# Gate-and-up product with four of eight pairs on seven products, a weight sum formed by an accumulating transfer, and the token scale folded into silu's result

## The chip, the cores and the metric

The kernel runs on one core of a Trainium2 chip. Its metric is the device time of one launch in microseconds (us). TensorE (PE) multiplies, VectorE (DVE) and ScalarE (ACT) work elementwise, GpSimd (POOL) here mostly issues transfers, and SyncE (SP) issues the loads. SBUF is the memory on the core; PSUM holds what PE sums up, in banks of 128 x 512 floats.

## The reference

A decoder of two layers on 256 tokens with 2048 features, all in float32. Layer 0 mixes tokens by a dilated sliding-window attention, layer 1 by a latent attention; the change leaves both alone. Each layer ends with a feed-forward block (FFN):

```python
def swiglu(xn, w_gu, w_down):
    g, u = jnp.split(xn @ w_gu, 2, axis=-1)
    return (jax.nn.silu(g) * u) @ w_down
...
h = h + swiglu(rms_norm(h, ffn_norm_g[layer]), ffn_w_gu[layer], ffn_w_down[layer])
```

`w_gu` is 2048 x 11264 (5632 columns of gate, then 5632 of up), `w_down` 5632 x 2048. `rms_norm` multiplies each token by one number, the token scale below.

## The kernel before

**Products.** Every float32 operand is split into two fp32r halves, `hi` (a rounded copy, by ACT) and `lo` (what is left, by DVE). A product of two blocks is then three matmuls: hi by hi, hi by lo, lo by hi (L595 to L597, called by `mul` in `mixed`). Each has 128 tokens against 512 weight columns.

**Weights.** `WeightStream` passes all weights through as units of 128 x 2048 floats (1 MB): rows 2kp and 2kp+1 (in blocks of 128) of two bands of 512 columns, one *pair* kp. `load` brings a unit into one of three `raw` buffers by transfers that SP issues; `split` makes `hi` and `lo` of it (L146 on ACT, L147 on DVE), two units ahead of use; `begin` does the first part of the third unit ahead (its early steps: the sums and the cast of `hi`).

**Eight or seven.** A pair is a 2 x 2 block product: two halves of the tokens, two bands of columns, two row blocks. In the form "eight" that is eight products, 24 matmuls, summed in two accumulators (`acc`, one for the gate or left band, one for the up or right band). In the form "seven" it is done by sums and differences with seven products, 21 matmuls. This needs sums of the weights (L168 adds two quarters of `raw` in place, L169 and L170 form three more, `sums`, by DVE), their halves `th` (ACT) and `tl` (DVE), sums of the activations (`forms`, `forms_h`, made by `sums`, L565 on), and four PSUM banks, `pb`, which gather over all seven-pairs of a group. After the last seven-pair the four banks are cast (L635 on ACT; L636, L637 and L642 on DVE) into the tiles `gate` and `up` (in down groups `left` and `right`). `raw` has three buffers, `hi` and `lo` three each, `th`, `tl` and `sums` one each.

**Groups.** One call of `mixed` is a group. `ffn` does the hidden columns in three parts of 16, 16 and 12 blocks (`FFN_PARTS`): first a gate-and-up group of eight pairs for every four blocks, then the down groups of that part. Per layer these are 11 gate-and-up groups and 5 down groups. The first gate-and-up group of a layer has eight products in every pair; the other ten have seven in the pairs of `SEVEN = (2, 4, 6)`. At a gate-and-up group's end, `close` adds the accumulator to what the banks gave (L861), ACT applies silu with the token scale (L866), and DVE multiplies `up` by the token scale and by `gate` (L870). One pair later (`later.put(1, turned)`) `turned` transposes `up` on PE (L429) into `hT`, the left operand of the down groups. Down groups end by adding into the residual `h`, one part by DVE, one by transfers on POOL's queue that add in memory (L890, to `h` from `gate` and `up`).

**Order.** In the FFN, DVE and ACT run in the order in which the code is written (`tc.manual_schedule(engines=ORDERED)`). PE's order is chosen by the scheduler of the framework. Units are numbered by their pair below: unit 1 of a group is the load of pair 1.

## Time and profile before

| | us |
|---|---|
| median of 3 runs (2654.10 to 2654.79) | 2654.57 |
| the profiled execution | 2654.07 |
| its span (first to last instruction) | 2652.0 |

| | busy us | share of the span |
|---|---|---|
| PE | 2637.8 | 99% |
| DVE | 2183.1 | 82% |
| ACT | 1324.0 | 50% |
| POOL | 29.7 | 1% |

The mean granted clock is 0.998. The loads move 492.65 MB and take 56.5% of the time of the 16 DMA engines; the queue that POOL feeds moves 10.49 MB. A gate-and-up group takes 42.67 us, a down group of eight pairs 41.70 us. The share of an engine is an average over the whole program, so the question of which engine has room has to be asked for a single group, where the change is.

### The profile page before, as it was taken

Reading aid. Unit: us, or ns where it says so; the run is one execution under the profiler, and the core shown is the slowest. Engines: PE = TensorE matmul, PEld = TensorE weight load, DVE = VectorE, ACT = ScalarE, POOL = GpSimd, SP = SyncE. Lnnn points to the kernel's source line nnn. Section 1 sums busy time; section 2 is a strip of 40 time slices with the busy share of each in tenths; the row PEclk is TensorE's granted clock in tenths of the full one; section 3 lists DMA queues with packets and bytes.
Section 4 is the critical chain, followed back from the end, with each engine's and each line's share of the span. In section 5 each row is a group of like instructions: output and inputs, shape, how many; then the busy total and the mean of one; then the engine's idle time right before and its main releaser. Section 6 shows DMA issues by size and latency. Waiting matters only on the chain.

```text
span 2652.0 us, 32612 instructions
## 1 busy us (share of the span) xinstructions
PE 2637.8 (99%) x12856; PEld 2214.1 (83%) x12856; DVE 2183.1 (82%) x2590; ACT 1324.0 (50%) x1404; POOL 29.7 (1%) x32
## 2 busy tenths in 40 slices
PE   9999999999999999999999999999999999999998
PEld 7888888888888888888888888888888888888887
DVE  6776777777677789998899898688789998998996
ACT  5444444534444455554554455565555554554554
POOL 0000000000000000000000000000000000000000
PEclk9999999999999999999999999999999999999999
DMA  7544645554554555567567757544565676657765
GB/s 263 188 165 160 206 159 175 186 180 159 174 189 161 191 185 197 190 209 235 191 198 218 219 181 223 166 152 136 159 206 180 201 222 207 207 183 230 217 209 159
DMA packets 310265, 506.27 MB, mean 191 GB/s; under 512 B 15112, under 2 KB 118240, under 8 KB 309728
## 3 DMA queue, kind: packets, MB, share of 16 engines
q1 hardware_dynamic: 304048, 492.65, 56.5%
q0 software_dynamic: 5440, 10.49, 2.5%
q8 instruction: 100, 1.64, 0.2%
q10 hardware_dynamic: 624, 1.07, 0.1%
q14 instruction: 53, 0.43, 0.0%
HBM read 491.57 MB, written 2.10 MB: 186 GB/s over the span
## 4 chain that ended last, share of the span: by engine, by line
PE 95%; DVE 2%; issue 1%; ACT 1%; DMA 1%; SPq 0%; POOL 0%; POOLq 0%; DVEq 0%; ACTq 0%
PE acc L595 16%; PE acc L596 16%; PE acc L597 16%; PE acc L489 15%; PE acc L492 8%; PE bank L597 4%; PE bank L595 4%; PE bank L596 3%; PE acc L509 3%; PE acc L510 3%; PE acc L508 3%; PE bank L429 1%; PE bank L689 1%; DVE lo L147 1%; PE bank L704 1%
## 5 line engine op out<-in xcount | busy, mean ns | idle before, releaser
L146 ACT CAST hi<-raw 128x2048 fp32r<-128x2048 f32 (+3 forms) x622 | 882.9, 1445 | 897.5 <-PE acc L489 268.7
L147 DVE TENSOR_TENSOR lo<-raw,hi 128x2048 fp32r<-128x2048 f32 (+3 forms) x622 | 1057.1, 1710 | 252.6 <-ACT hi L146 228.2
L595 PE MATMUL acc<-hi,xT_f 128*128 128x512 f32 x996 | 391.1, 393 | 0.0
L596 PE MATMUL acc<-lo,xT_f 128*128 128x512 f32 x996 | 389.3, 391 | 0.0
L597 PE MATMUL acc<-hi,xT_f 128*128 128x512 f32 x996 | 388.3, 390 | 0.0
L489 PE MATMUL acc<-xT_a,hi 128*128 128x512 f32 x1536 | 379.1, 396 | 0.0
L489 PEld LDWEIGHTS acc<-xT_a,hi 128*128 128x128 f32 x1536 | 281.8, 188 | 53.7
L595 PEld LDWEIGHTS acc<-hi,xT_f 128*128 128x128 f32 x996 | 187.1, 188 | 40.5 <-ACT gate L866 0.8
L597 PEld LDWEIGHTS acc<-hi,xT_f 128*128 128x128 f32 x996 | 187.1, 188 | 39.8
L596 PEld LDWEIGHTS acc<-lo,xT_f 128*128 128x128 f32 x996 | 187.1, 188 | 39.0 <-DVE lo L147 0.4
L147 DVE TENSOR_TENSOR tl<-sums,th 128x1536 fp32r<-128x1536 f32 x104 | 182.4, 1754 | 39.7 <-ACT th L146 39.7
L492 PEld LDWEIGHTS acc<-xT_a,lo 128*128 128x128 f32 x1536 | 196.9, 191 | 7.5
L492 PE MATMUL acc<-xT_a,lo 128*128 128x256 f32 x1536 | 199.3, 283 | 0.0
L146 ACT CAST th<-sums 128x1536 fp32r<-128x1536 f32 x104 | 154.2, 1483 | 67.6 <-PE acc L597 45.2
L595 PE MATMUL acc<-hi,hT 128*128 128x512 f32 x412 | 161.4, 392 | 0.0
L596 PE MATMUL acc<-lo,hT 128*128 128x512 f32 x412 | 160.9, 391 | 0.0
L597 PE MATMUL acc<-hi,hT 128*128 128x512 f32 x412 | 160.7, 390 | 0.0
L170 DVE TENSOR_TENSOR sums<-raw,sums 128x1024 f32<-128x1024 f32 x104 | 127.4, 1225 | 3.4
L595 PEld LDWEIGHTS acc<-hi,hT 128*128 128x128 f32 x412 | 77.4, 188 | 16.5
L597 PEld LDWEIGHTS acc<-hi,hT 128*128 128x128 f32 x412 | 77.4, 188 | 16.4
L596 PEld LDWEIGHTS acc<-lo,hT 128*128 128x128 f32 x412 | 77.4, 188 | 16.1
L508 PE MATMUL acc<-hi,xT_a 128*128 128x512 f32 x192 | 76.6, 399 | 0.0
(341 smaller groups left out, 4053.4 us busy)
## 6 DMA issues: line engine op xcount, KB each, us to landing
raw<-in_ffn_w_gu_dram SPq DMA_DIRECT2D x352, 512.0 KB, 4.5
raw<-in_a_w_qkv_dram SPq DMA_DIRECT2D x119, 1024.0 KB, 4.8
raw<-in_ffn_w_down_dram SPq DMA_DIRECT2D x152, 512.0 KB, 4.7
raw<-in_a_w_qkv_dram SPq DMA_DIRECT2D x50, 512.0 KB, 4.6
raw<-in_a_w_o_dram SPq DMA_DIRECT2D x32, 512.0 KB, 4.8
raw<-in_b_w_o_dram SPq DMA_DIRECT2D x32, 512.0 KB, 4.6
raw<-in_ffn_w_down_dram SPq DMA_DIRECT2D x12, 1024.0 KB, 6.4
raw<-in_b_w_kv_b_dram SPq DMA_DIRECT2D x8, 1024.0 KB, 5.2
```

The lines of the kernel that those rows point to most:

```text
L146: cast = lambda: nc.scalar.copy(out=hi, in_=src)
L147: rest = lambda: nc.vector.tensor_tensor(out=lo, in0=src, in1=hi.bitcast(F32), op=ALU.subtract)
L170: tt(out=w[:, 0::2], in0=v[:, 1::2], in1=w[:, 1].unsqueeze(1).broadcast_to([P, 2, 512]), op=ALU.subtract)
L429: nc.tensor.transpose(out=ps[:, jj * S + t * P:jj * S + (t + 1) * P], in_=srcs[t][:, (j + jj) * P:(j + jj + 1) * P], identity=ident)
L489: mm(out=acc[:, i, :], lhsT=sl(hi, kk), rhs=xT[:, k0 + kk, :], start=first and kk == 0, stop=False)
L492: mm(out=acc[:, i, 0:S], lhsT=sl(lo, kk), rhs=xT[:, k0 + kk, 0:S], start=False, stop=last and kk == nk - 1)
L508: mm(out=acc[:, t, :ncol], lhsT=xh, rhs=rhs(hi, kk), start=st, stop=False)
L509: mm(out=acc[:, t, :ncol], lhsT=xh, rhs=rhs(lo, kk), start=False, stop=False)
L510: mm(out=acc[:, t, :ncol], lhsT=xl, rhs=rhs(hi, kk), start=False, stop=sp)
L595: mm(out=out, lhsT=xh, rhs=wh, start=st, stop=False)
L596: mm(out=out, lhsT=xh, rhs=wl, start=False, stop=False)
L597: mm(out=out, lhsT=xl, rhs=wh, start=False, stop=sp)
```

## The change

It has four parts.

1. `SEVEN` becomes (1, 3, 5, 6): in the ten groups of a layer, four of eight pairs have seven products, 60 matmuls fewer in the whole program. Pairs 5 and 6 follow one another. Where the next pair is a seven too, `mixed` runs the products of the sums first (`summed`, then `plain`).
2. Seven-units of gate-and-up and of down get the form "summed": DVE's add of two quarters (L168) goes. SP loads three pieces (256, 512 and 256 KB), and a fourth transfer, issued by POOL, adds 256 KB from HBM to the first piece where it lies in `raw` (L110 to L113 of the changed kernel; 108 such transfers). The attention's output units keep the add.
3. The cast of the banks keeps its intermediate sum in a small tile `mid`, so `gate` shrinks from three parts of 512 to two, and the last step becomes two subtractions of 512 columns (L652) in place of one of 1024.
4. The token scale goes from DVE to ACT: L870 is gone, ACT multiplies silu's result by the scale (L884, two instructions), and a plain multiply of `up` by `gate` on DVE (L891) stands at the head of `turned`, one pair later than L870 stood. In a layer's first group, which has no L877 (the addition that was L861), ACT copies `up` out of PSUM.

```diff
--- before.py
+++ after.py
@@ -45,7 +45,7 @@
 C_M0, C_M1, C_M2, C_CA, C_SA, C_END = 1024, 1536, 1792, 2048, 2304, 2560
 
 
-SEVEN = (2, 4, 6)
+SEVEN = (1, 3, 5, 6)
 ORDERED = {mybir.EngineType.DVE, mybir.EngineType.Activation}
 SEVEN_O = (4, 6)
 SEVEN_V = ((), (2, 4, 6), (2, 4, 6), (4, 6))
@@ -104,9 +104,14 @@
         while self.n_raw < min(upto, len(self.units)):
             ap, _, form = self.units[self.n_raw]
             t = self.raw_pool.tile([P, 2048], F32, tag="raw", name="raw", bufs=self.raw_bufs)
-            if form in ("eight", "seven"):
+            if form in ("eight", "seven", "summed"):
                 v = t.rearrange("p (k n c) -> p k n c", n=2, c=512)
-                for n in range(2):
+                if form == "summed":
+                    self.nc.sync.dma_start(out=v[:, 0, 0, :], in_=ap[1][:, 0, :])
+                    self.nc.sync.dma_start(out=v[:, :, 1, :], in_=ap[0])
+                    self.nc.sync.dma_start(out=v[:, 1, 0, :], in_=ap[1][:, 1, :])
+                    self.nc.gpsimd.dma_start(out=v[:, 0, 0, :], in_=ap[0][:, 0, :], accum_op=ALU.add)
+                for n in range(0 if form == "summed" else 2):
                     self.nc.sync.dma_start(out=v[:, :, 1 - n, :], in_=ap[n])
                 self.raws[self.n_raw] = t
                 self.n_raw += 1
@@ -158,14 +163,15 @@
         hi, lo = [self.hl_pool.tile([P, 2048], F32R, tag=n, name=n, bufs=self.ahead + 1) for n in ("hi", "lo")]
         if form == "eight":
             return (hi, lo), self.halve(hi, lo, raw)
-        if form == "seven":
+        if form in ("seven", "summed"):
             th, tl = [self.sum_pool.tile([P, 1536], F32R, tag=n, name=n, bufs=1) for n in ("th", "tl")]
             sums = self.sum_pool.tile([P, 1536], F32, tag="sums", name="sums", bufs=1)
             v, w = [t.rearrange("p (i c) -> p i c", c=512) for t in (raw, sums)]
             tt = self.nc.vector.tensor_tensor
 
             def add():
-                tt(out=v[:, 0], in0=v[:, 0], in1=v[:, 1], op=ALU.add)
+                if form == "seven":
+                    tt(out=v[:, 0], in0=v[:, 0], in1=v[:, 1], op=ALU.add)
                 tt(out=w[:, 1], in0=v[:, 0], in1=v[:, 2], op=ALU.subtract)
                 tt(out=w[:, 0::2], in0=v[:, 1::2], in1=w[:, 1].unsqueeze(1).broadcast_to([P, 2, 512]),
                    op=ALU.subtract)
@@ -350,13 +356,13 @@
             for j in range(k0, k0 + n, 4):
                 for kp in range(KD // 2):
                     blocks = [v[:, 2 * kp:2 * kp + 2, b + j * P:b + j * P + 512] for b in (0, FF)]
-                    units.append((blocks, None, "seven" if j > 0 and kp in SEVEN else "eight"))
+                    units.append((blocks, None, "summed" if j > 0 and kp in SEVEN else "eight"))
             v = ffn_w_down[layer].rearrange("(k p) c -> p k c", p=P)
             paired = D // 2 if k0 + n == KF else D
             for c in range(0, paired, 1024):
                 for kp in range(n // 2):
                     blocks = [v[:, k0 + 2 * kp:k0 + 2 * kp + 2, b:b + 512] for b in (c, c + 512)]
-                    units.append((blocks, None, "seven" if kp in SEVEN_DOWN[n] else "eight"))
+                    units.append((blocks, None, "summed" if kp in SEVEN_DOWN[n] else "eight"))
             for c in range(paired, D, 512):
                 for k in range(k0, k0 + n, 4):
                     add_unit(ffn_w_down[layer], k, 4, c, 512)
@@ -609,13 +615,19 @@
                     pb = [bank() for _ in range(4)]
                 at = sums_of.shape[3] - 4
                 y = lambda j: x(1, 0) if j + at < 0 else [sums_of[:, i, h, j + at, :] for h in range(2)]
-                mul(pb[0], x(0, 0), w[:2], 1, st, sp)
-                mul(la[:, 0], x(0, 1), w[:2], 3, first("la0"), False)
-                mul(pb[1], y(0), w[:2], 0, st, sp)
-                mul(ra[:, 0], y(3), w[:2], 2, first("ra0"), False)
-                mul(pb[3], y(2), w[2:], 0, st, sp)
-                mul(pb[2], y(1), w[2:], 1, st, sp)
-                mul(la[:, 1], x(1, 1), w[2:], 2, first("la1"), False)
+                def plain():
+                    mul(pb[0], x(0, 0), w[:2], 1, st, sp)
+                    mul(la[:, 0], x(0, 1), w[:2], 3, first("la0"), False)
+                    mul(pb[1], y(0), w[:2], 0, st, sp)
+                    mul(ra[:, 0], y(3), w[:2], 2, first("ra0"), False)
+
+                def summed():
+                    mul(pb[3], y(2), w[2:], 0, st, sp)
+                    mul(pb[2], y(1), w[2:], 1, st, sp)
+                    mul(la[:, 1], x(1, 1), w[2:], 2, first("la1"), False)
+
+                for part in (summed, plain) if kp + 1 in seven else (plain, summed):
+                    part()
             else:
                 for i, (acc, m) in enumerate(((la, "la"), (ra, "ra"))):
                     for t in range(NT):
@@ -838,7 +850,11 @@
                     sums(xT, kp, forms[:, SEVEN.index(kp)])
 
             def pair_tiles():
-                return [fp.tile([P, n, 512], F32, tag=m, name=m) for m, n in (("gate", NT + 1), ("up", NT))]
+                return [fp.tile([P, NT, 512], F32, tag=m, name=m) for m in ("gate", "up")]
+
+            def pieces(left, right):
+                mid = tmp.tile([P, 2, S], F32, tag="t1", name="mid").rearrange("p a b -> p (a b)")
+                return [left[:, 0], mid, left[:, 1]], right
 
             for part, (k0, n) in enumerate(FFN_PARTS):
                 last = part == len(FFN_PARTS) - 1
@@ -855,7 +871,7 @@
                             later.put(kp + 3, lambda kp=kp: scaled(kp))
                     sc_ = rstd if first else rem
 
-                    def close(i, acc, first=first, both=(gate[:, 0:3:2], up), sc_=sc_):
+                    def close(i, acc, first=first, both=(gate, up), sc_=sc_):
                         d = both[i]
                         if not first:
                             nc.vector.tensor_tensor(out=d, in0=acc, in1=d, op=ALU.add)
@@ -864,18 +880,20 @@
                         def silu():
                             for t in range(NT):
                                 nc.scalar.activation(out=d[:, t], in_=acc[:, t], func=AF.Silu, scale=sc_[:, t:t + 1])
+                            for t in range(NT):
+                                nc.scalar.activation(out=d[:, t], in_=d[:, t], func=AF.Copy, scale=sc_[:, t:t + 1])
                         if i == 0:
                             return silu
-                        for t in range(NT):
-                            nc.vector.scalar_tensor_tensor(out=d[:, t], in0=acc[:, t], scalar=sc_[:, t:t + 1],
-                                                           in1=both[0][:, t], op0=ALU.mult, op1=ALU.mult)
-
-                    def turned(j=j, up=up, hT=hT, seven=SEVEN_DOWN[n], sums_h=sums_h):
+                        if first:
+                            nc.scalar.copy(out=d, in_=acc)
+
+                    def turned(j=j, gate=gate, up=up, hT=hT, seven=SEVEN_DOWN[n], sums_h=sums_h):
+                        nc.vector.tensor_tensor(out=up, in0=up, in1=gate, op=ALU.mult)
                         transposed([up[:, t, :] for t in range(NT)], hT, j, None)
                         for kp in (j // 2, j // 2 + 1):
                             if kp in seven:
                                 sums(hT, kp, sums_h[:, seven.index(kp)])
-                    mixed(xT, KD // 2, () if first else SEVEN, forms, lambda gate=gate, up=up: (gate, up), close)
+                    mixed(xT, KD // 2, () if first else SEVEN, forms, lambda gate=gate, up=up: pieces(gate, up), close)
                     later.put(1, turned)
 
                 for c in range(0, 2 if last else 4, 2):
@@ -885,8 +903,8 @@
                         d = chunks(c + i)
                         nc.vector.tensor_tensor(out=d, in0=acc, in1=d, op=ALU.add)
 
-                    mixed(hT, n // 2, SEVEN_DOWN[n], sums_h, lambda left=left, right=right: (left, right), close)
-                    for i, part_sum in enumerate((left[:, 0:3:2], right)):
+                    mixed(hT, n // 2, SEVEN_DOWN[n], sums_h, lambda left=left, right=right: pieces(left, right), close)
+                    for i, part_sum in enumerate((left, right)):
                         nc.gpsimd.dma_start(out=chunks(c + i), in_=part_sum,
                                             accum_op=ALU.add)
                     if last:
```

What this does to DVE's order where one gate-and-up group (with seven-pairs) meets the next. Before, from the last cast of the banks on (in all such rows: line, operation, output, inputs, shape):

```order
L636 TENSOR_TENSOR gate<-bank,gate 128x512
L637 TENSOR_TENSOR gate<-bank,gate 128x512
L642 TENSOR_TENSOR up<-bank,gate 128x1024
L861 TENSOR_TENSOR gate<-acc,gate 128x2x512
L147 TENSOR_TENSOR lo<-raw,hi 128x2048
L861 TENSOR_TENSOR up<-acc,up 128x1024
L870 SCALAR_TENSOR_TENSOR up<-up,rem,gate 128x512 x2
L168 TENSOR_TENSOR raw<-raw 128x512
L169 TENSOR_TENSOR sums<-raw 128x512
L170 TENSOR_TENSOR sums<-raw,sums 128x2x512
```

Of the changed kernel, DVE at the same place, from the second cast of the banks to the first work after the transposes:

```order
L649 TENSOR_TENSOR gate<-bank,mid 128x512
L652 TENSOR_TENSOR up<-bank,mid 128x512
L652 TENSOR_TENSOR up<-bank,gate 128x512
L175 TENSOR_TENSOR sums<-raw 128x512
L176 TENSOR_TENSOR sums<-raw,sums 128x2x512
L877 TENSOR_TENSOR gate<-acc,gate 128x1024
L152 TENSOR_TENSOR lo<-raw,hi 128x2048
L152 TENSOR_TENSOR tl<-sums,th 128x1536
L877 TENSOR_TENSOR up<-acc,up 128x1024
L152 TENSOR_TENSOR lo<-raw,hi 128x2048
L175 TENSOR_TENSOR sums<-raw 128x512
L176 TENSOR_TENSOR sums<-raw,sums 128x2x512
```

Behind these stands L891, the multiply that completes `up`. So between the addition of `up` and the end of `up` there were no other instructions, and now there are a `lo` (unit 2) and the sums of unit 3; the sums and `tl` of unit 1 stand ahead of them, between the casts of the banks and the addition of `up`.

On PE, whose rows here carry the numbers of the tiles, the rows around the transposes of `up` at such a place were these. `acc_8723` and `acc_8724` are the new group's accumulators, `hi_8643` its unit 0, `hi_8675` its unit 1:

```order
L596 MATMUL acc_8724<-lo_8644,xT_f0_7039 128x512
L597 MATMUL acc_8724<-hi_8643,xT_f0_7039 128x512
L429 MATMUL bank_8758<-ident_95,up_8416 128x128 x4
L429 MATMUL bank_8765<-ident_95,up_8416 128x128 x4
L595 MATMUL acc_8723<-hi_8675,xT_f0_7039 128x512
L596 MATMUL acc_8723<-lo_8676,xT_f0_7039 128x512
```

In the changed kernel the transposes (`up_8445`) come later. The new group's unit 0 is `hi_8679`, unit 1 `hi_8715` with `th_8717`, unit 2 `hi_8759`:

```order
L603 MATMUL acc_8764<-hi_8679,xT_f0_7039 128x512
L601 MATMUL acc_8764<-hi_8715,xT_f0_7039 128x512
L602 MATMUL acc_8764<-lo_8716,xT_f0_7039 128x512
L603 MATMUL acc_8764<-hi_8715,xT_f0_7039 128x512
L601 MATMUL acc_8764<-th_8717,xT_f0_7039 128x512
L602 MATMUL acc_8764<-tl_8718,xT_f0_7039 128x512
L603 MATMUL acc_8764<-th_8717,xT_f0_7039 128x512
L601 MATMUL acc_8764<-hi_8759,xT_f0_7039 128x512
L601 MATMUL acc_8765<-hi_8679,xT_f0_7039 128x512
```

Matmuls of units 1 and 2 that need no bank of `pb` were moved ahead into unit 0's: 42 matmuls stand between the group's first one and the transposes, where 24 stood before.

On ACT the same place was, before, from the cast of a bank on:

```order
L635 COPY gate<-bank 128x512
L146 CAST hi<-raw 128x2048
L866 ACTIVATE gate<-gate,rem 128x512 x2
L146 CAST hi<-raw 128x2048
L146 CAST th<-sums 128x1536
```

And in the changed kernel:

```order
L647 COPY gate<-bank 128x512
L151 CAST hi<-raw 128x2048
L151 CAST th<-sums 128x1536
L882 ACTIVATE gate<-gate,rem 128x512 x2
L884 ACTIVATE gate<-gate,rem 128x512 x2
L151 CAST hi<-raw 128x2048 x2
```

A `th` of unit 1 now stands ahead of silu, and the two multiplies by the token scale behind it, ahead of the `hi` of units 2 and 3.

## The prediction

> **What bounds the kernel now.** I read the page first: its busy line, the slices and the chain.
>
> ```profile
> span 2652.0 us, 32612 instructions
> ...
> PE 2637.8 (99%) x12856; PEld 2214.1 (83%) x12856; DVE 2183.1 (82%) x2590; ACT 1324.0 (50%) x1404; POOL 29.7 (1%) x32
> ...
> DVE  6776777777677789998899898688789998998996
> ...
> PE 95%; DVE 2%; issue 1%; ACT 1%; DMA 1%; SPq 0%; POOL 0%; POOLq 0%; DVEq 0%; ACTq 0%
> ```
>
> PE bounds: it makes 95% of the chain. But DVE reaches nine tenths in the slices of the FFN, so I took the busy time of single groups: first a gate-and-up group (from one L635 copy to the next), then a down group.
>
> ```profile
> 1304.07:1346.74 42.67, 42.67 (x193) 35.20 (x192) 40.38 (x36) 23.06 (x20) 0.00 (x0) 1.00 0.60 196
> 1432.10:1473.80 41.70, 41.70 (x184) 34.33 (x183) 35.77 (x25) 19.81 (x13) 2.40 (x2) 1.00 0.78 231
> ```
>
> Columns are length, PE, PEld, DVE, ACT, POOL, clock, DMA share, GB/s. In gate-and-up DVE works 40.38 of 42.67 us; in down it has 6 us to spare. The clock is 1.00, and DMA is at 0.60 to 0.78. So DVE has some 2 us a group left, just where the change adds to it. Next I looked at where two gate-and-up groups meet, first PE.
>
> ```profile
> 1306.12 0.39 PE L595 MATMUL acc<-th,xT_f 128*128 128x512 f32 x1
> ...
> 1312.08 0.39 PE L597 MATMUL acc<-hi,xT_f 128*128 128x512 f32 x1
> 1312.30 0.39 PE L595 MATMUL acc<-hi,xT_f 128*128 128x512 f32 x1
> ...
> 1317.75 1.03 PE L429 MATMUL bank<-ident,up 128*128 128x128 f32 x8
> ```
>
> From 1306.12 to 1317.75 lie 51 matmuls (3, then 24 and 24): **0.228 us** each. The next group begins at 1312.30, which I call **E**. Its first 24 matmuls run, then the eight transposes of the old group's `up`, at E+5.45, without a wait. DVE at the same place:
>
> ```profile
> 1304.20 2.29 DVE L147 TENSOR_TENSOR lo<-raw,hi 128x2048 fp32r<-128x2048 f32 x1 [1.81 <-ACT hi L146]
> 1306.41 0.68 DVE L636 TENSOR_TENSOR gate<-bank,gate 128x512 f32<-128x512 f32 x1
> 1307.13 0.69 DVE L637 TENSOR_TENSOR gate<-bank,gate 128x512 f32<-128x512 f32 x1
> 1307.85 1.22 DVE L642 TENSOR_TENSOR up<-bank,gate 128x1024 f32<-128x1024 f32 x1
> 1309.78 1.23 DVE L861 TENSOR_TENSOR gate<-acc,gate 128x1024 f32<-128x1024 f32 x1 [0.71 <-PE acc L597]
> 1310.92 2.28 DVE L147 TENSOR_TENSOR lo<-raw,hi 128x2048 fp32r<-128x2048 f32 x1
> 1313.12 1.22 DVE L861 TENSOR_TENSOR up<-acc,up 128x1024 f32<-128x1024 f32 x1
> 1314.44 1.42 DVE L870 SCALAR_TENSOR_TENSOR up<-up,rem,gate 128x512 f32<-128x512 f32 x2
> 1315.78 0.68 DVE L168 TENSOR_TENSOR raw<-raw 128x512 f32<-128x512 f32 x1
> 1316.49 0.69 DVE L169 TENSOR_TENSOR sums<-raw 128x512 f32<-128x512 f32 x1
> 1317.22 1.23 DVE L170 TENSOR_TENSOR sums<-raw,sums 128x1024 f32<-128x1024 f32 x1
> ```
>
> `up` is finished at 1315.86, 1.9 us before PE wants it. From start to start these cost: 0.72 for 512 columns, 1.14 to 1.2 for 1024 (1.27 for L170 with its wait), 2.20 for a `lo`. That spare 1.9 us is what the change spends.
>
> **The change part by part.** *Products.* Each of the 10 changed groups a layer, 20 in all, loses one product of three matmuls: 60 x 0.228 = **-13.6 us**, if PE stays fed. It is the only gain on PE's path.
>
> *DVE's load.* A gate-and-up group loses three raw adds (L168) and gains a fourth pair's sums (0.69 + 1.23) and `tl`:
>
> ```profile
> L147 DVE TENSOR_TENSOR tl<-sums,th 128x1536 fp32r<-128x1536 f32 x104 | 182.4, 1754 | 39.7 <-ACT th L146 39.7
> L146 ACT CAST th<-sums 128x1536 fp32r<-128x1536 f32 x104 | 154.2, 1483 | 67.6 <-PE acc L597 45.2 <-DVE lo L147 18.9 <-DVE sums L170 0.5
> L866 ACT ACTIVATE gate<-gate,rem 128x512 f32<-128x512 f32 x40 | 26.8, 718 | 80.4 <-DVE gate L861 80.4
> ```
>
> 40.38 - 3 x 0.68 + 0.69 + 1.23 + 1.75 + 0.15 (`right` in two halves) - 0.2 (L870's pair becomes one multiply) = 41.96 us, against PE's 42.67 - 0.68 = 41.99. The slack is gone. In down DVE only loses work, which PE covers.
>
> *Where the work lands.* Unit k is the load of pair k. With pair 1 instead of pair 2 in the list, the next group's unit 1 needs sums and `tl` while the old group closes, and L891, the multiply before the transposes, now follows unit 2's `lo` and unit 3's sums (the order rows of DVE above). The chain's start comes first. Unit 6's `th` shares its one buffer with unit 5's, so ACT may write it only after nine matmuls of unit 5, which begins 66 matmuls (15.0 us) before E. These rows price the rest:
>
> ```profile
> 1302.25 1.91 ACT L146 CAST hi<-raw 128x2048 fp32r<-128x2048 f32 x1 [2.19 <-PE acc L597]
> 1311.10 1.34 ACT L866 ACTIVATE gate<-gate,rem 128x512 f32<-128x512 f32 x2 [4.24 <-DVE gate L861]
> 1318.48 1.49 ACT L146 CAST th<-sums 128x1536 fp32r<-128x1536 f32 x1
> 1319.87 1.91 ACT L146 CAST hi<-raw 128x2048 fp32r<-128x2048 f32 x1
> ```
>
> E-15.0 + 2.05 + 0.25 (PE to reader, as 1309.53 to 1309.78 at L861) = E-12.7; `th` and unit 7's `hi` 1.39 + 1.91, two `lo` 4.4: DVE starts the eviction at **E-5.0**, not at E-5.9 as now. Then four evictions 2.88, unit 1's sums 1.99, gate's add 1.14, unit 1's `lo` 2.20 and `tl` 1.67, up's add 1.2, unit 2's `lo` 2.20, unit 3's sums 1.99, L891 1.22: 16.5 us, so `up` is ready at E+11.5. PE has been given 42 matmuls to run ahead of the transposes (counted in its order; 24 before), 9.55 us. It stands for 2.0 us, plus 0.1 for the signal; ACT's `hi` of unit 2, behind two silus and two new copies, ends at about E+5.9 and costs nothing more. After the transposes unit 1 at once wants all four PSUM banks, two of them still being cast: 0 to 0.45, I take 0.3. **2.4 us at each of 14 joints** (7 a layer). Bounds: 1.2, if the chain starts at E-5.9 as now, and 4.4, if a transfer adds 2 us (below).
>
> *Other joints.* Gate to down: no unit-1 sums, but unit 2's sums, `lo` and `tl` stand before L891: 14.5 us from E-5.0 against the same 42 matmuls: 0.3 at six joints. Down to gate: the chain starts at E-5.9 and has no L891; gate's buffer comes free at E+0.2: 0.3 at four. Down to down: hidden.
>
> *First group to second,* once a layer. In this place now:
>
> ```profile
> 1008.65 1.22 DVE L478 TENSOR_TENSOR xT_f<-xT_f,R 128x1024 fp32r<-128x1024 f32 x1
> ...
> 1012.49 0.56 DVE L405 TENSOR_TENSOR forms<-g,forms 128x384 fp32r<-128x384 f32 x1
> 1012.97 2.29 DVE L147 TENSOR_TENSOR lo<-raw,hi 128x2048 fp32r<-128x2048 f32 x1
> 1015.40 1.41 DVE L870 SCALAR_TENSOR_TENSOR up<-acc,rstd,gate 128x512 f32<-128x512 f32 x2 [0.15 <-PE acc L597]
> ```
>
> Scaling one pair and forming its sums takes 4.3 us (1008.65 to 1012.97). L870 ran at 1015.40, ahead of pairs 5 and 6; L891 stands behind the scaling of 3 to 6 with the sums of 3, 5 and 6. By the same prices it ends near 1032.5, where PE, with 59 matmuls from 1015, is ready at about 1028.5; `lo` and `tl` of units 3 to 5 then run late by 0.3 to 1 each. I take **6 us** (bounds 3 and 8), twice.
>
> *The accumulating transfer.* No row shows one from HBM, so I bound it by these:
>
> ```profile
> raw<-in_b_w_kv_a_dram SPq DMA_DIRECT2D x2, 256.0 KB, 2.7
> h<-gate POOLq DMA_DIRECT2D x10, 512.0 KB, 5.9
> h<-up POOLq DMA_DIRECT2D x10, 512.0 KB, 9.5
> L890 POOL DMA_DIRECT2D h<-gate x10 | 12.2, 1218 | 1295.3 <-DVE h L886 700.9 <-issue 594.3
> ```
>
> The first piece lands after 2.7 us, then POOL issues: at most 5.9 us with twice the bytes; less half of the 3.6 us that the second 512 KB adds, 4.1. So 6.8 to 8.6 us from a free buffer to a summed one. The shortest windows from the `lo` that frees it to the first sum are unit 1's (`tl`, two `lo`, four evictions: 9.0) and unit 6's (9.7). It fits, barely: cost 0; with 11 us it would be 2 a joint. Behind the two transfers to `h` (9.5 us, from E+2) unit 4's sum in the second down group lands near E+16; its products begin at E+21, so PE does not notice.
>
> POOL's issue took 1218 ns on average with DVE at work around it; nothing in that row says that DVE holds it up. Here a rule speaks against the change: the Trainium skill, "SBUF — State Buffer", section "Who interferes with whom", says that transfers whose descriptors GpSimd writes wait while DVE holds the port pair that both share, and also that `tensor_tensor`, which is what DVE runs in these stretches, was not seen to stall them. By its first half each issue could slip by up to the 2.29 us of a `lo`, and the third rival's time would come out; by its second half, and by the row, it costs nothing, which is what the sum has.
>
> A second rule bears on the gaps. The granted clock is 1.00 in both group rows above. The Trainium skill, "TensorE: Matmul & The Clock Gate", section "HAM oscillation — how this bites in real kernels", says that TensorE, idle for more than about 3.4 us, falls to half clock, and the section on the gate that it needs about as long to come back. By it the two first groups alone could be hit, if their wait came in one piece: half of 3.4 us lost at each, an estimate of 2692 us instead of my sum. No row of the FFN shows such a gap, so the sum leaves it out.
>
> **Sum.** -13.6 + 14 x 2.4 + 6 x 0.3 + 4 x 0.3 + 2 x 6 = **+35**. The profiled execution took 2654.07 us (its span of 2652.0 and 2.07 around it), 0.5 under the median of the runs shown, so I predict **2689 us**.
>
> **Rivals.** *PE's gain alone*: the moved matmuls cover the whole chain, and 2654.1 - 13.6 = 2640 comes out, faster. It holds if `up` is ready by E+9.5, two microseconds earlier than I find, and if the first groups hide their chain too. For it speaks that PE's order carries 18 more matmuls as cover, and that DVE's load, 41.96 us, still fits PE's 41.99; against it the 16.5 us of rows without a gap. 0.15. *A draw*: joints of about 1 us (DVE starting at E-5.9, the first groups at 1 or 2 us) give back just the gain, 2649 to 2660: 0.1. *A late sum*: first piece, issue and accumulation take some 11 us instead of 8, DVE waits 2 us at each of the 14 joints, +28: 2717. It decides above a window of 9.0 us; the 9.5 us landing of the second transfer to `h` speaks for it, the 5.9 us of the first against it. 0.18. That the change doesn't do what it says is excluded by the order: 60 matmuls fewer.
>
> **How the numbers follow.** Forecast 0.57, late sum 0.18, draw 0.1, gain 0.15. The low end is the draw's, 2649; the forecast with its joints at their lower bounds (1.2 and 3) is 2666. The high end, 2723, is the late sum and a little above; outside lie the gain and the late sum's tail. A measurement here can tell about 0.2%, 5.3 us. Slower by more than that: 0.75; within: 0.1; faster: 0.15.
>
> **What would show it.** Right: gate-and-up groups 44 to 45 us apart instead of 42.67; the transposes of `up` waiting for DVE's L891; DVE over 93% busy in these groups; down groups still 41.8. Wrong: groups at 42.0 (then the cover suffices), or DVE's sums and ACT's `hi` waiting for the transfer on POOL's queue (then the late sum holds).

## The result and the profile after

The changed kernel takes **2705.43 us** (median of four runs, 2699.81 to 2706.38) against 2654.65 us before: 1.0186 times as long, with a 95% interval of 1.0173 to 1.0199. The forecast was 2689 us, slower, in a range of 2649 to 2723.

These are the lines of the page of the changed kernel that answer to those shown of before: span, busy time, DVE's slices and the chain.

```profile
span 2704.2 us, 33193 instructions
...
PE 2653.4 (98%) x12796; PEld 2201.3 (81%) x12796; DVE 2186.9 (81%) x2584; ACT 1380.0 (51%) x1474; POOL 123.3 (5%) x140
...
DVE  6777776777677789988998887688788988988896
...
PE 63%; DVE 14%; DMA 12%; issue 5%; ACT 5%; SPq 0%; ACTq 0%; POOL 0%; POOLq 0%; DVEq 0%
```

PE has its 60 matmuls fewer (12796 against 12856), and yet its part of the chain fell from 95% to 63%: DVE, DMA and ACT now stand between PE's pieces. Busy shares say nothing of this; DVE's even fell.

The windows of single groups, taken as before from one copy of a bank to the next: a quiet gate-and-up group, the worst one, one followed by a down group, and a down group.

```profile
1317.30:1360.99 43.69, 43.10 (x189) 34.30 (x189) 41.38 (x37) 25.45 (x23) 2.90 (x4) 1.00 0.72 211
2049.55:2098.00 48.45, 43.65 (x188) 35.16 (x187) 41.22 (x37) 25.35 (x22) 3.45 (x4) 0.96 0.66 195
1404.70:1449.48 44.78, 43.77 (x194) 35.27 (x194) 37.65 (x34) 24.19 (x22) 2.58 (x3) 1.00 0.69 200
1449.48:1490.70 41.22, 41.22 (x182) 33.61 (x181) 34.32 (x24) 19.88 (x14) 5.88 (x6) 1.00 0.93 267
```

The stretch into a down group was this before:

```profile
1389.40:1432.07 42.67, 42.67 (x193) 35.19 (x192) 40.38 (x36) 23.07 (x19) 0.00 (x0) 1.00 0.62 197
```

Even the quiet group takes 43.69 us where 41.99 would do for PE; DVE is at work in 41.38 of it, 95%. In the stretch into a down group DVE works less than before, 37.65 us against 40.38, and it still takes 2.1 us longer; the down group behind it loses nothing. The waits of PE and of DVE over the whole program (in all, times, longest):

```profile
PE acc L601 <- DVE gate L877: 17.3, 14, 4.8
PE bank L435 <- DVE up L891: 9.3, 8, 1.9
...
DVE sums L175 <- DMA raw<-in_ffn_w_down_dram: 37.1, 16, 3.8
DVE hT L411 <- ACT hT L410: 34.0, 23, 2.4
...
DVE sums L175 <- DMA raw<-in_ffn_w_gu_dram: 19.9, 9, 3.8
```

PE's longest wait is for L877 of `gate`: the addition that closes the old group's gate accumulator, whose buffer the new group needs. The prediction had looked for the wait at the transposes (L891); of PE's eight waits for L891 only one stands at a gate-to-gate joint (0.5 us), and five at joints into down (1.0 to 1.9 us). Two of DVE's waits are new: for the accumulating transfers (L175), and 34.0 us for `hT`. Here is DVE at the quiet joint. E, from which PE was free for the new group, is 1325.15 (its last matmul of the old group began at 1324.92, and 0.228 us); its first matmul of the new one began at 1325.77.

```profile
1320.03 0.69 DVE L648 TENSOR_TENSOR mid<-bank,gate 128x512 f32<-128x512 f32 x1
...
1324.41 1.22 DVE L877 TENSOR_TENSOR gate<-acc,gate 128x1024 f32<-128x1024 f32 x1
...
1334.61 1.22 DVE L891 TENSOR_TENSOR up<-up,gate 128x1024 f32<-128x1024 f32 x1
1337.33 1.29 DVE L411 TENSOR_TENSOR hT<-bank,hT 128x512 fp32r<-128x512 f32 x2 [1.51 <-ACT hT L410]
```

The casts begin at E-5.1, `gate` is closed at E+0.5, `up` is ready at E+10.7. Then DVE stands still for 1.51 us: its next instruction needs what PE transposes and ACT casts out of the `up` that DVE has only just written.

### The profile page after: what moved, and what is told of

Same layout as the page of the kernel before. It is cut to its first block, busy times and chain, and to the rows that moved or that the text cites. A ratio compares the mean times of both kernels' runs of the same rounds, so it can differ in the third digit from the quotient of the medians.

```text
span 2704.2 us, 33193 instructions
## 1 busy us (share of the span) xinstructions
PE 2653.4 (98%) x12796; PEld 2201.3 (81%) x12796; DVE 2186.9 (81%) x2584; ACT 1380.0 (51%) x1474; POOL 123.3 (5%) x140
## 4 chain that ended last, share of the span: by engine, by line
PE 63%; DVE 14%; DMA 12%; issue 5%; ACT 5%; SPq 0%; ACTq 0%; POOL 0%; POOLq 0%; DVEq 0%
PE acc L495 14%; DMA raw<-in_ffn_w_gu_dram 8%; PE acc L601 8%; PE acc L498 7%; PE acc L602 7%; PE acc L603 7%; DVE lo L152 6%; ACT hi L151 3%; DMA raw<-in_ffn_w_down_dram 3%; PE acc L516 3%; PE acc L515 3%; PE acc L514 3%; PE bank L602 2%; PE bank L603 2%; PE bank L601 2%
## 5 line engine op out<-in xcount | busy, mean ns | idle before, releaser
L601 PE MATMUL acc<-hi,xT_f 128*128 128x512 f32 x856 | 336.9, 397 | 21.6 <-DVE gate L877 17.3
L602 PE MATMUL acc<-lo,xT_f 128*128 128x512 f32 x856 | 335.6, 392 | 1.0 <-DVE lo L152 1.0
L603 PE MATMUL acc<-hi,xT_f 128*128 128x512 f32 x856 | 334.8, 391 | 0.0
L151 ACT CAST th<-sums 128x1536 fp32r<-128x1536 f32 x124 | 183.7, 1482 | 173.5 <-DVE sums L176 88.2
L152 DVE TENSOR_TENSOR tl<-sums,th 128x1536 fp32r<-128x1536 f32 x124 | 217.3, 1752 | 25.9 <-ACT th L151 25.1
L601 PEld LDWEIGHTS acc<-hi,xT_f 128*128 128x128 f32 x856 | 161.1, 188 | 69.2 <-issue 23.3
L602 PEld LDWEIGHTS acc<-lo,xT_f 128*128 128x128 f32 x856 | 161.3, 188 | 35.2 <-DVE lo L152 1.9
L603 PEld LDWEIGHTS acc<-hi,xT_f 128*128 128x128 f32 x856 | 161.2, 188 | 35.2
L176 DVE TENSOR_TENSOR sums<-raw,sums 128x1024 f32<-128x1024 f32 x124 | 151.9, 1225 | 4.2
L175 DVE TENSOR_TENSOR sums<-raw 128x512 f32<-128x512 f32 x124 | 85.3, 688 | 74.1 <-DMA raw<-in_ffn_w_down_dram 37.1
L113 POOL DMA_DIRECT2D raw<-in_ffn_w_gu_dram x80 | 69.4, 867 | 833.9 <-DMA raw<-in_ffn_w_gu_dram 474.4
L601 PEld LDWEIGHTS acc<-hi,hT 128*128 128x128 f32 x412 | 77.6, 188 | 18.3 <-DVE h L904 1.2
```

Of the source, the lines that this page charges most:

```text
L151: cast = lambda: nc.scalar.copy(out=hi, in_=src)
L152: rest = lambda: nc.vector.tensor_tensor(out=lo, in0=src, in1=hi.bitcast(F32), op=ALU.subtract)
L175: tt(out=w[:, 1], in0=v[:, 0], in1=v[:, 2], op=ALU.subtract)
L176: tt(out=w[:, 0::2], in0=v[:, 1::2], in1=w[:, 1].unsqueeze(1).broadcast_to([P, 2, 512]), op=ALU.subtract)
L601: mm(out=out, lhsT=xh, rhs=wh, start=st, stop=False)
L602: mm(out=out, lhsT=xh, rhs=wl, start=False, stop=False)
```

## The experiments

Besides the times, this table splits each profiled execution at the copies of a bank (L647 on ACT): the mean of the 14 stretches from a gate-and-up group to the next, the sum of the six that lead into a down group, the sum of the eight that begin in a down group, and what the two stretches that hold the first groups (from the program's start, and from layer 0's last copy to layer 1's first) take more than before.

```
                            median us  gate-gate  gate-down  down   first groups
before                      2654.65    42.68      235.8      334.0     0
changed                     2705.43    44.77      251.5      332.0   +10.0
E1 no accumulating transfer 2674.88    43.68      236.3      333.3    +7.1
E2 gate closes first        2726.06    44.94      250.8      332.6   +25.7
E3 multiply in close        2673.39    43.61      234.1      333.1    +7.3
E4 three pairs              2661.88    42.65      242.2      333.4    +2.9
E5 multiply ahead of sums   2690.08    43.87      246.8      334.7    +5.9
E6 E1 and E3                2669.71    43.57      233.6      333.3    +5.7
E7 before, scale only       2667.40    43.17      240.1      334.0    +0.8
E8 before, transfer only    2654.43    42.65      235.5      334.0    +0.4
E9 four pairs only          2698.65    45.25      234.6      334.2    +9.8
E10 E3 with 2, 4, 5, 6      2661.29    42.45      233.2      334.6    +9.4
E11 multiply on POOL        2702.14    45.56      237.2      332.8    +7.0
E12 E10 mended              2650.74    42.39      233.1      335.7    +2.2
```

**E1, no accumulating transfer.** The transfer is left out and nothing put in its place:

```diff
-                    self.nc.gpsimd.dma_start(out=v[:, 0, 0, :], in_=ap[0][:, 0, :], accum_op=ALU.add)
```

> The changed kernel without the 108 accumulating transfers: the quarter of the weights that they would add is left out, so the sums are made from what SP loads alone; every other instruction stays. Theory ORDER (DVE's list at the joints and its full load make the loss; the transfers are hidden): the joints keep their waits, and the time stays within 5 us of 2705. Theory LATE SUM (where the sum of unit 1 or unit 6 has to wait for its transfer, DVE's whole list slips and PE with it): in the trace of the changed kernel the sums L175 wait for a landing 34 times, some 69 us of DVE in all, and those gate-and-up joints at which it waits cost PE 2.5 to 6.5 us where undisturbed ones cost 1.7. With all 14 at 1.7 (24 us), the two first groups still at some 5, and PE's gain of 13.6: 2675 to 2685. I expect 2680.

2674.88 us, at the lower edge of what LATE SUM gave. Without transfers no sum waits, and 30.5 us go, half at the gate-to-gate joints (14 x 1.09 us), half at the six joints into down (15.2 us). So LATE SUM holds for these 30 us. The remaining 20 us are no transfer's.

**E2, gate closes first.**

```diff
-            ws.begin()
+            if not (seven and kp == pairs - 2):
+                ws.begin()
```

> The changed kernel with one call moved: the early steps of the next group's unit 1 (its sums on DVE, its hi on ACT) are issued behind the addition that closes the gate accumulator, not ahead of it. Theory ORDER: PE's wait for that addition (L877 of gate, 17 us in 14 places) goes, part of it comes back at th, tl and hi of unit 1 and at the transposes, which still wait for the same list; 2690 to 2697. Theory LATE SUM: where the transfer is late, PE no longer waits for it through the gate accumulator and has unit 0's 24 matmuls to run, so the long waits of 2 to 5 us go too; 2680 to 2690. If what PE waits for is DVE's total load, not the place in its list, 2700 to 2706.

2726.06 us, outside all three. The wait for L877 of `gate` is gone from the list, and this stands in its place:

```profile
PE acc L602 <- DVE lo L152: 12.8, 14, 1.8
PE acc L602 <- DVE tl L152: 9.6, 14, 0.7
PE bank L435 <- DVE up L892: 8.6, 6, 1.6
```

A wait that leaves one place in DVE's list comes back at the next. The gate-to-gate stretches did not shorten (44.94 against 44.77). Most of the 21 us lost lie in the stretches with the first groups (25.7 against 10.0): the edit also acts on the attention's output and the down groups, which I had not separated out, so E2 says nothing about those.

**E3, the multiply in close.** The first `turned` line goes, and `close` ends with:

```diff
-                        if first:
-                            nc.scalar.copy(out=d, in_=acc)
+                        nc.vector.tensor_tensor(out=d, in0=acc, in1=both[0], op=ALU.mult)
```

> The changed kernel with the multiply of up by gate back where the two scaled multiplies stood before, right behind the addition of up (in the first groups out of PSUM, without ACT's copy of up). My prediction's step (the transposes wait for this multiply, 2.0 us at each of 14 joints) would make this 2705 - 25 = 2680. What the trace of the changed kernel shows is 11.6 us of waiting at the transposes, and the gate's wait ahead of it, which this edit leaves: by that, 2693 to 2698.

2673.39 us, below either figure but closer to the first, and not for the reason that I gave: the transfers are still late (DVE waits for them in 15 + 9 places), but at the joints into down PE no longer notices (234.1 against 251.5). What is left of PE's wait for the closing addition is this:

```profile
PE acc L601 <- DVE gate L877: 10.1, 14, 1.7
```

**E4, three pairs.**

```diff
-SEVEN = (1, 3, 5, 6)
+SEVEN = (2, 4, 6)
```

> The changed kernel with seven products in the pairs 2, 4 and 6, as before the change; transfers, pieces and token scale stay changed. PE has its 60 matmuls again (+13.6 us), DVE loses 3 x 0.68 us a group and has 4 us of room. Theory ORDER: without sums of unit 1 at the joint, and with that room, no joint waits; 2652 to 2658. Theory LATE SUM: the windows of units 2, 4 and 6 are no longer than those of 1, 3, 5 and 6, so late landings still stop DVE now and then, but it has room to catch up; up to 2665. Above 2670 the transfer would be the cause in itself, whatever the pairs.

2661.88 us, 1.0025 (1.0016 to 1.0035) of before. That lies in the range of LATE SUM. Gate to gate it is as fast as before, 42.65 us; most of the loss is in the joints into down (242.2 against 235.8). There the multiply is late and the sum ahead of it may be late, as in the changed kernel.

**E5, two instructions exchanged.** The multiply is issued just ahead of `ws.begin()`, so it stands before the sums of unit 3 on DVE, not after them.

```diff
+            for fn in soon:
+                fn()
+            soon.clear()
             ws.begin()
             later.tick()
...
-                        nc.vector.tensor_tensor(out=up, in0=up, in1=gate, op=ALU.mult)
...
+                    soon.append(lambda gate=gate, up=up: nc.vector.tensor_tensor(out=up, in0=up, in1=gate, op=ALU.mult))
                     later.put(1, turned)
```

> The changed kernel with the multiply of up by gate two places earlier in DVE's list, ahead of the sums of unit 3 in place of behind them; two instructions change places, nothing else. A new theory, TURNAROUND: in the changed kernel DVE waits 34.0 us, 23 times, for hT (L411 behind ACT's cast, L410), and not at all before the change. The multiply stands right ahead of the cast's other half in DVE's list, and between the two PE must transpose and ACT must cast, some 1.45 us, in which DVE, whose list of 41.96 us has no room, does nothing. With the sums (1.99 us) between them that hole is filled: 20 to 24 times 1.4, so 2672 to 2680. Rival, theory LATE MULTIPLY (my prediction's: PE waits at the transposes): only the waits at the transposes go, 11.6 us, 2693 to 2698.

2690.08 us, between the two. TURNAROUND gets part of it: the hole shrank from 34.0 us to this,

```profile
DVE hT L412 <- ACT hT L411: 14.1, 20, 1.4
```

and the gate-to-gate stretches fell by 0.9 us each. The edit also takes the multiply out from behind a sum that may be late, so this run alone does not say which of the two helped (E6 bears on it). And the 16.7 us between this kernel and E3 are still there, and 12.7 of them in the joints into down (246.8 against 234.1).

**E6, the edits of E1 and E3 together,** as shown there.

> The changed kernel with both edits that each took some 31 us: no accumulating transfers (their quarter of the weights is left out) and the multiply in close. If the two losses are apart, 2705 - 31 - 31 = 2643, near PE's gain alone (2640). If both are the same loss, DVE without room, that shows only when two things come together, 2665 to 2673: DVE's 41.4 us a group, with its remaining waits, then still sets a period of 43 to 43.5 against PE's 41.99. I expect 2660.

2669.71 us, in the range for one and the same loss. With E1 and E3 this makes a square: late multiply and transfers 2705.4; late multiply alone 2674.9; transfers alone 2673.4; neither 2669.7. Each alone costs 4 to 5 us, the two together 36. The joint into down shows how, in the changed kernel, DVE first, then PE:

```profile
1413.47 1.22 DVE L877 TENSOR_TENSOR up<-acc,up 128x1024 f32<-128x1024 f32 x1
1416.06 0.69 DVE L175 TENSOR_TENSOR sums<-raw 128x512 f32<-128x512 f32 x1 [1.37 <-DMA raw<-in_ffn_w_down_dram]
...
1421.93 1.22 DVE L891 TENSOR_TENSOR up<-up,gate 128x1024 f32<-128x1024 f32 x1
...
1423.20 1.09 PE L435 MATMUL bank<-ident,up 128*128 128x128 f32 x8 [0.99 <-DVE up L891]
```

The sum waits for its transfer, and the multiply that PE needs is queued behind it, although `up` was complete from 1414.69. With the multiply in close the same late sum has nothing behind it that PE is waiting for.

E1 and E6 also bear on TURNAROUND, since E1 has the hole and E6 has not. Of DVE's waits, E1 first, then E6:

```profile
DVE tl L151 <- ACT th L150: 53.9, 33, 2.1
DVE hT L410 <- ACT hT L409: 34.9, 22, 2.0
```

```profile
DVE tl L151 <- ACT th L150: 74.1, 51, 2.1
```

The hole of 34.9 us is gone in E6, DVE waits 20 us more for `th` instead, and a gate-to-gate stretch is only 0.11 us shorter (43.57 against 43.68). So where no transfer is late, filling the hole gains little: another wait takes its place.

**E7, the kernel before with the token scale on ACT and the late multiply only.**

```diff
                                 nc.scalar.activation(out=d[:, t], in_=acc[:, t], func=AF.Silu, scale=sc_[:, t:t + 1])
+                            for t in range(NT):
+                                nc.scalar.activation(out=d[:, t], in_=d[:, t], func=AF.Copy, scale=sc_[:, t:t + 1])
...
-                            nc.vector.scalar_tensor_tensor(out=d[:, t], in0=acc[:, t], scalar=sc_[:, t:t + 1],
-                                                           in1=both[0][:, t], op0=ALU.mult, op1=ALU.mult)
...
+                        nc.vector.tensor_tensor(out=up, in0=up, in1=gate[:, 0:3:2], op=ALU.mult)
```

> The kernel before with one part of the change: token scale on ACT, the plain multiply at the head of turned. DVE has 42.67 - 40.4 us of room in a group. TURNAROUND: the 1.45 us hole takes most of that room; the multiply also stands behind a lo and a tl now, so the transposes wait where nothing was moved ahead of them: up to 2 us at each of 14 joints; 2660 to 2680. If the fold costs nothing while DVE has room, 2652 to 2657.

2667.40 us, 12 us more than before, with the hole in DVE's list that the kernel before has not:

```profile
DVE hT L405 <- ACT hT L404: 30.8, 22, 1.6
```

PE's list names a late `lo` here, and not the multiply, which fits a DVE that has fallen behind:

```profile
PE acc L596 <- DVE lo L147: 4.5, 8, 0.8
```

The hole and the late place of the multiply come together in this run, so it does not show the share of either.

**E8, the kernel before with the accumulating transfer only,** in the pairs 2, 4 and 6 (here the core; the forms of the units follow it).

```diff
+                if form == "summed":
+                    self.nc.sync.dma_start(out=v[:, 0, 0, :], in_=ap[1][:, 0, :])
+                    self.nc.sync.dma_start(out=v[:, :, 1, :], in_=ap[0])
+                    self.nc.sync.dma_start(out=v[:, 1, 0, :], in_=ap[1][:, 1, :])
+                    self.nc.gpsimd.dma_start(out=v[:, 0, 0, :], in_=ap[0][:, 0, :], accum_op=ALU.add)
...
-                tt(out=v[:, 0], in0=v[:, 0], in1=v[:, 1], op=ALU.add)
+                if form == "seven":
+                    tt(out=v[:, 0], in0=v[:, 0], in1=v[:, 1], op=ALU.add)
```

> The kernel before with one part of the change: the accumulating transfer in place of DVE's add, in the same pairs 2, 4 and 6 (88 transfers). DVE gains 3 x 0.68 us of room in a gate-and-up group. The transfers land 7.5 to 14 us after the buffer is free, some late, but DVE has 4.3 us of room to make up for it and PE is the bound: 2652 to 2657. If late sums reach PE by themselves: 2658 to 2665.

2654.43 us, 0.9998 (0.9988 to 1.0007) of before: nothing. The landings are late here too (`sums <- DMA` 40 us in ten places), and with DVE's room, and no multiply for PE behind these sums, they cost nothing.

**E9, four pairs only.** DVE's add and the two scaled multiplies are back; four pairs and the pieces stay.

```diff
-                    units.append((blocks, None, "summed" if j > 0 and kp in SEVEN else "eight"))
+                    units.append((blocks, None, "seven" if j > 0 and kp in SEVEN else "eight"))
...
-                            for t in range(NT):
-                                nc.scalar.activation(out=d[:, t], in_=d[:, t], func=AF.Copy, scale=sc_[:, t:t + 1])
...
-                        if first:
-                            nc.scalar.copy(out=d, in_=acc)
+                        for t in range(NT):
+                            nc.vector.scalar_tensor_tensor(out=d[:, t], in0=acc[:, t], scalar=sc_[:, t:t + 1],
+                                                           in1=both[0][:, t], op0=ALU.mult, op1=ALU.mult)
...
-                        nc.vector.tensor_tensor(out=up, in0=up, in1=gate, op=ALU.mult)
```

> The changed kernel without two of its parts: DVE's add in place of the accumulating transfer (gate-and-up and down), and the token scale back in DVE's two scaled multiplies in close. So it is the kernel before with four pairs of seven products and the cast in pieces. Theory DVE BOUND: a gate-and-up group takes what DVE works plus the 1.5 to 2 us that it must wait in it for th. Here DVE works 41.96 + 4 x 0.68 + 0.2 = 44.9 us, so 46.4 to 46.9 us a group where PE needs 41.99, at the 14 joints with another gate-and-up group some 4.6 us each, at the six others and the first groups 10 to 20 more: 2654 - 13.6 + 65 + 15 = 2715 to 2730. If PE's order, not DVE's load, bounds these groups, it would be near the 2670 of the kernels with the multiply in close.

2698.65 us: slower by 43 us, and less than I expected. DVE BOUND had the kind right and the size wrong. A group, by its window:

```profile
1100.80:1146.55 45.75, 43.93 (x194) 35.06 (x193) 44.33 (x42) 24.22 (x20) 0.00 (x0) 1.00 0.53 181
```

DVE works 44.33 of 45.75 us. The wait for `th` that I had added to its work does not add: when DVE is later, ACT is ready (in the 14 gate-to-gate stretches `tl` waits for it 2.7 us in all, against 18.7 in E3).

**E10, pairs 2, 4, 5, 6, multiply in close.** E3, and:

```diff
-SEVEN = (1, 3, 5, 6)
+SEVEN = (2, 4, 5, 6)
```

> The changed kernel with the multiply in close and the pairs 2, 4, 5 and 6 in place of 1, 3, 5 and 6: as many matmuls, as much work of DVE, but no sums of unit 1 between the casts of the banks and the addition that frees the gate accumulator. Theory ORDER: the wait of PE for that addition (10.1 us with the multiply in close and the pairs 1, 3, 5 and 6) goes; 2655 to 2663. Theory DVE BOUND: 41.5 us of work and the waits for th, of which three adjoining sevens make more, still set the period: 2670 to 2685. I expect 2670.

2661.29 us, 1.0023 (1.0014 to 1.0032). DVE works as much as in E3, but a group takes 42.34 us and not 43.51. E3's group first, then E10's:

```profile
1309.60:1353.11 43.51, 42.93 (x190) 34.29 (x189) 41.47 (x37) 25.43 (x22) 3.44 (x4) 1.00 0.73 217
```

```profile
1096.90:1139.24 42.34, 42.34 (x190) 34.56 (x189) 41.44 (x37) 25.57 (x23) 3.49 (x4) 1.00 0.74 221
```

So with the same load 1.2 us a group hang on where the sums stand. ORDER's range holds, not the 2670 that I expected: PE's wait for the closing addition fell from 10.1 us to 1.6.

```profile
PE acc L601 <- DVE gate L877: 1.6, 2, 0.8
```

DVE's time not at work fell with it, from 2.04 to 0.90 us in these two groups. Other sums moved too, so the whole 1.2 us cannot be put down to unit 1's alone.

**E11, the multiply on POOL.** Against E3:

```diff
-                        nc.vector.tensor_tensor(out=d, in0=acc, in1=both[0], op=ALU.mult)
+                        eng = nc.vector if first else nc.gpsimd
+                        eng.tensor_tensor(out=d, in0=acc, in1=both[0], op=ALU.mult)
```

> The changed kernel with the multiply of up by gate in close, and there on POOL in place of DVE (all groups but the first of a layer). DVE works 1.2 us less a group. Theory DVE BOUND: the period falls from 43.5 us by that 1.2 to some 42.3, against 2673 with DVE's multiply in close: 18 groups x 1.2 = 20 us, 2652 to 2656. Against it: POOL's multiply may take several times DVE's 1.2 us, so that the transposes wait for it, and the accumulating transfers behind it in POOL's list start later, which with a full DVE reaches PE: 2680 to 2700.

2702.14 us: the second case. POOL takes three times as long as DVE's 1.22 us, and the transposes wait for it:

```profile
L888 POOL TENSOR_TENSOR up<-up,gate 128x1024 f32<-128x1024 f32 x20 | 73.7, 3683 | 94.0 <-DVE up L877 94.0
```

```profile
PE bank L435 <- POOL up L888: 16.8, 14, 1.4
```

**E12, a mended version.** E10, with two edits:

```diff
-SEVEN = (1, 3, 5, 6)
+SEVEN = (2, 4, 5, 6)
+SEVEN_2 = (2, 4, 6)
...
-                    units.append((blocks, None, "summed" if j > 0 and kp in SEVEN else "eight"))
+                    units.append((blocks, None, "summed" if j > 0 and kp in (SEVEN if k0 + j > 4 else SEVEN_2) else "eight"))
...
-                    units.append((blocks, None, "summed" if kp in SEVEN_DOWN[n] else "eight"))
+                    units.append((blocks, None, "seven" if kp in SEVEN_DOWN[n] else "eight"))
...
+                        later.put(14, lambda: sums(xT, 5, forms[:, 3]))
```

> The kernel with the multiply in close and the pairs 2, 4, 5 and 6, with two more edits: the second gate-and-up group of each layer has seven products in the pairs 2, 4 and 6 alone (the sums of the activations of pair 5 are made five pairs later), and the down groups have DVE's add back, with no accumulating transfer. In the profile of the kernel with 2, 4, 5 and 6 the first and second group of a layer take 93.8 us together against 88.9 before, 9.8 us in all, and the down groups behind gate-and-up groups and behind each other some 3 us more than PE needs. If these are the first groups' sums and the late landings in down, they go: -8.4 and -3 from 2661, so 2648 to 2652, under the kernel before (2655). If the first groups' loss comes from the fold or the transfers and not from the fourth pair, 2656 to 2660.

2650.74 us, 0.9985 of before (0.9976 to 0.9994): faster than both kernels, by a little. The first groups' loss fell from 9.4 to 2.2 us. Down did not shorten (335.7 against 334.6), so the second half of that expectation fell.

## Why the prediction came out as it did

The direction and the kind of cause held: DVE's list at the joints, not PE, sets the time. The forecast loss was 35 us, the measured one 51. Of the signs that it named, groups 44 to 45 us apart, DVE over 93% busy and unharmed down groups came true; the wait of the transposes came at other joints than it said, and the sign against it, sums waiting for the transfer, came too. By its own terms:

- **PE's gain, -13.6 us.** Right: 60 matmuls went. E12, without 54 of them, keeps some of it: 42.39 us a gate-to-gate stretch, where 42.68 was before and 41.99 would do for PE.
- **Gate to gate, 14 x 2.4 = 33.6 us.** Measured: 44.77 - 41.99 = 2.8 each, 39 in all. The DVE chain was right to 1 us (casts from E-5.1 for E-5.0, `up` at E+10.7 for E+11.5), the place of the wait was not. I followed the list to the transposes and never asked, at this joint, who waits for the closing addition of `gate`, though by my own prices it ended at E+1.0; PE stopped there first, and then waited at the transposes at one of the 14 joints only (at the quiet one it came to them at E+10.9, when `up` was ready). That 2.4 and 2.8 lie so close is luck: the wait that was priced did not happen, and others of about its size did. Without the transfers a joint loses 43.68 - 41.99 = 1.7 (E1); the other 1.1 is late landing. Of E3's 1.6, E10 takes away 1.2 by moving the sums.
- **Gate to down, 6 x 0.3 = 1.8 us.** This is the step that failed. Measured: 251.5 - 235.8 = 15.7, or 2.6 each. (These stretches have none of PE's gain: they hold the products of a down group, and the matmuls that went are missing in the stretches that end in a gate-and-up group.) The prediction put the sums of unit 2 ahead of L891 and priced them as if their data were there; it weighed late sums only as a rival, and only at the 14 gate-to-gate joints. E1, E3 and E6 show that the late landing and the late multiply cost this together: with either one gone the six stretches take 236.3 or 234.1 us. It is not DVE's load: in the stretch shown that is 37.65 us, where PE needs 42.67.
- **Down to gate, 4 x 0.3 = 1.2 us.** Held: 332.0 - (334.0 - 4 x 0.68) = 0.7 over the eight stretches that begin in a down group.
- **DVE's load, 41.96 us in PE's 41.99.** The sum was near (41.38 measured), the conclusion not drawn. I counted what DVE does and not what it must wait for: the 1.5 us between L891 and L411, 34.0 us in all, is absent from the prediction. That L870 before stood well ahead of the transposes was its cover. How much of the 51 us this hole makes is not shown: E7 has it and loses 12 us, but with the late multiply; E1 has it and E6 has not, and they differ by 5.2 us.
- **First groups, 2 x 6 = 12 us.** Measured 10.0, or 11.4 with the 2 x 0.68 us that PE needs less there. The size was right, the wait was not: L891 ended where the prediction had it (near 1032), but PE stood for it 0.8 us at each of the two, and the loss stays with the multiply in close (9.4 in E10). With three pairs it is 2.9 (E4), and 2.2 where only the second group has three (E12): it is the fourth pair's.
- **The transfer, 6.8 to 8.6 us from a free buffer to a summed one, cost 0.** From the issue of the first piece to the landing, the trace has a median of 9.0 us for gate and up and 10.9 for down, and up to 15.0. The rival of the late sum (28 us, given 0.18) came close in price: E1 takes away 30.5, but half of that at the joints into down, which the rival did not name. It was wrong in its condition, since E8 has late landings too and loses nothing. They cost where work that PE waits for is queued behind the sum, as E4 shows even with three pairs.
- **PE's gain alone, and the draw,** fell, as argued.

The three parts by themselves: transfer 0 (E8), scale with the late multiply +12 (E7), four pairs +43 (E9). The transfer, with the scale on ACT, pays back 25 us of the four pairs' 43 by taking work off DVE (E3 against E9); the late multiply takes 32 away again (the changed kernel against E3). Not settled is why the landings at the gate-to-gate joints are later with the late multiply (DVE's sums wait 17 us there in the changed kernel and 7 in E3): both issue the same transfers, and no run separates their timing.

## What to carry to other kernels

An engine with a fixed order has less room than its busy time says: to its work belong the turnarounds that its own list forces, where an instruction stands right behind the one that feeds it through other engines. What filling such a hole gains has to be tried, since the next wait may take its place (E1 and E6). In such a list, put the instruction that the bounding engine waits for ahead of every one that may itself wait for a transfer. When an engine's load reaches the bound's, ask at each joint for every result, not only for the last, who is waiting for it.

## What the hardware did that I had not expected

**The clock.** The prediction left a slower clock out. At the worst joint of the changed kernel PE waited 4.80 us, and then the matmuls followed each other not in 0.228 us but in 0.43:

```profile
2061.55 0.76 PE L601 MATMUL acc<-hi,xT_f 128*128 128x512 f32 x1 [4.80 <-DVE gate L877]
2062.11 0.63 PE L602 MATMUL acc<-lo,xT_f 128*128 128x512 f32 x1
2062.54 0.63 PE L603 MATMUL acc<-hi,xT_f 128*128 128x512 f32 x1
...
2064.25 0.62 PE L601 MATMUL acc<-hi,xT_f 128*128 128x512 f32 x1
2064.68 0.42 PE L602 MATMUL acc<-lo,xT_f 128*128 128x512 f32 x1
```

```profile
2061.50:2065.00 3.50, 3.45 (x9) 2.76 (x10) 3.50 (x2) 3.50 (x6) 0.00 (x0) 0.54 0.42 62
```

The granted clock of that stretch is 0.54. The changed kernel has three such stretches (from 1621.8, 2061.6 and 2424.4 us), 21 matmuls of some 0.2 us more each, about 4 us of its 51; the kernel before has none in its FFN, and neither have E1, E3, E6, E10 and E12. So, by these profiled executions, some 4 of the 31 us that E1 or E3 takes away are the clock's. The Trainium skill, "TensorE: Matmul & The Clock Gate", section "HAM oscillation — how this bites in real kernels", tells of this with a gap of over 3.4 us. The trace agrees on the half rate; on the length it differs: in E5 a gap of 2.61 us between two starts (from 2044.19) was followed by such a stretch, 1 us after PE had gone on, and in the changed kernel one of 3.03 us at 1107.19 was followed by none.

**The accumulating transfer.** POOL's issue took 867 ns on average and 1.06 us at most, and began some 0.6 us (median) after the first piece had landed, so it did not slip behind DVE:

```profile
L113 POOL DMA_DIRECT2D raw<-in_ffn_w_gu_dram x80 | 69.4, 867 | 833.9 <-DMA raw<-in_ffn_w_gu_dram 474.4
```

So the slip of up to 2.29 us an issue that was weighed ahead of the run did not come. The landings were late where loads ran beside them. Of the 108 transfers, the 29 with no load of the next unit (two of 512 KB on SP's queue) issued from 2.2 us ahead to 2.5 us behind them landed after 4.2 us (median, 4.0 to 5.5); the 67 with both halves of one landed after 5.9 us, the last after 9.2.
